# Two buffers for the shifted copies and banded weights of a convolution on TensorE, its steps placed differently among the projection tiles

## The chip, the core and the metric

The kernel runs on one core of one Trainium2 chip. The metric is the device time of one execution in microseconds (us). Before the change the median of three runs is 1551.79 us (1549.15 to 1553.39).

## The reference

One inference step of a two-layer encoder for 512 prompt frames and 8 x 16 sample frames, 640 columns in all. Layer 0 is a convolution module and a SwiGLU block; layer 1 projects keys and values, attends, and has a SwiGLU block too. The change touches the convolution module:

```python
def conv_module(h, hist, g, w_pw1, b_pw1, w_dw, b_dw, ln_g, ln_b, w_pw2, b_pw2):
    a, gate = jnp.split(rms_norm(h, g) @ w_pw1 + b_pw1, 2, axis=-1)
    glu = a * jax.nn.sigmoid(gate)
    full = jnp.concatenate([hist.astype(glu.dtype), glu], axis=1)
    y = lax.conv_general_dilated(
        full, w_dw[:, None, :].astype(full.dtype), window_strides=(1,), padding="VALID",
        dimension_numbers=("NWC", "WIO", "NWC"), feature_group_count=D_MODEL) + b_dw
    y = jax.nn.silu(layer_norm(y, ln_g, ln_b))
    return h + y @ w_pw2 + b_pw2, full[:, -CONV_HIST:]
def swiglu_ffn(h, g, w_in, w_out):
    a, b = jnp.split(rms_norm(h, g) @ w_in, 2, axis=-1)
    return h + (jax.nn.silu(a) * b) @ w_out
```

The model width is 1024 (8 chunks of 128 channels), the convolution has 31 taps for each channel, all arrays are float32.

## The kernel before

**Columns and products.** Channels lie on the 128 partitions, frames on the free axis. The 640 columns are two groups: g0 with 256 (the samples and the first 128 prompt frames) and g1 with 384. A float32 product is made of three matmuls (`mm3`, lines 167 to 172): weights and data are split into a high and a low part, and L170 is high by high, L171 low weights by high data, L172 high weights by low data. A weight tile (2048 columns, 1 MB) is loaded by SyncE (SP) into `raw` (L134, L139); ScalarE (ACT) makes its high part `whi` (L150), and VectorE (DVE), GpSimd (POOL) or both make its low part `wlo` (L154). `raw`, `whi` and `wlo` have two buffers each.

**Steps.** The order of the first part of layer 0 is the string `PLAN` (line 70). A loop at the end of the quoted code runs its tokens through `step`:

- aN, bN: tile N of the first projection for g0 or g1: two accumulations of 24 matmuls, 256 or 384 columns wide; then tanh and bias on ACT (L380, L383) and the gated product on DVE, written with the history to `gs` (g0) or `gp` (g1, L395).
- lgN, pgN: chunk N of the convolution of group g on TensorE (PE). l makes the banded weights `w4` on POOL (L444), copies the chunk to DRAM (`sc`, L452) and reads it back as four shifted copies `x4` by four DMAs of SP (L455, 368 KB each for g0). p is 32 groups of four small matmuls (L469) and a copy to `y` on ACT (L471).
- dg..: chunks convolved on DVE, one instruction for each tap (L434 for the first, L437 for the others), with the sums in PSUM and a copy to `y` on ACT (L440).
- qgN: a chunk convolved on ACT (L416) and POOL (L417).
- ng: the layer norm of the convolution. POOL adds seven chunks (L195), PE makes the sum over the partitions (L204), DVE copies it, PE spreads it over the partitions (L216); L483 subtracts the mean. Squares (L179) are added in the same way, L226 and L230 make the reciprocal root, PE spreads it again, L489 scales, L491 is the silu on ACT, and L159 and L160 split the result into the high and low data of the second projection.
- wg: the second projection, four weight tiles, 192 matmuls for g0; L506 adds to `h`.
- rg: the norm ahead of the SwiGLU block. For g0: squares, POOL sums, the sum on PE, L226, L230, the spread, then L243 (DVE), L159 and L160 for each of 8 chunks.
- f: one chunk of that block for g0, six input tiles (`ffn_in`; L287 silu, L288 product, L160) and the output tiles (`ffn_out`, L303). With a weight tile of f, POOL makes three quarters of `wlo` and DVE one quarter.
- x, y, s: norm and load of g1, and a store of the new history.

The five p steps are chunks 4, 5, 7 and 6 of g0 (in this order) and chunk 3 of g1.

**Who sets the order.** Each engine runs its instructions in its own order. The tile framework's scheduler makes that order from the code's order, with priorities (the blocks under `high_priority`) and a simulated timeline; so an engine's order follows `PLAN` only in the large. The pools wait for buffers: a tile with one buffer can't be written until the last reader of the tile before it has ended. `w4` and `x4` are in pool `cp`, which has one buffer for a tag. PSUM has four buffers for accumulations.

Of the kernel before, what the change touches and what calls it, by code (L numbers as in the profile page):

```python
# [8 lines left out]
F32 = mybir.dt.float32  # L9
# [5 lines left out]
P = 128  # L15
# [14 lines left out]
GSW = 16 * SEG + 4  # L30
# [36 lines left out]
FG = (1, 0)  # L67
SSQ1 = 'ppapappp'
LNO = ((1, 5, 4, 3, 6, 0, 2, 7), (3, 5, 6, 4, 2, 7, 1, 0))
PLAN = ("a0 y a1 a2 a4 x a3 a5 a6 l04 p04 l05 d0213 a7 b0 p05 b1 l07 p07 l06 b2 q00 s0 p06 n0 b3 b4 b5 d145 l13 w0 b7 r0 p13 b6 f q16 s1 d101 d127 n1 f f w1 r1")  # L70

V_NCONV, V_BPW1, V_BDW, V_LNG, V_LNB, V_BPW2 = 0, 8, 24, 32, 40, 48
V_NKV, V_NATT, V_NFFN, V_NFIN, V_N = 56, 64, 72, 88, 96
# [4 lines left out]
def tile_trunk(ctx, tc, xT, vecs, hist, w_pw1, w_pw2, w_in0, w_out0, w_in1, w_out1,  # L78
# [13 lines left out]
    def nm(s):  # L92
        uid[0] += 1
        return f"{s}_{uid[0]}"
# [241 lines left out]
    cp = cv.enter_context(tc.tile_pool(name="cp", bufs=1))  # L336
# [19 lines left out]
    for b in range(2, 4):  # L356
        nc.gpsimd.tensor_tensor(out=i4, in0=i4, in1=ident[:, 32 * b:32 * b + 32], op=ALU.add)
    y0 = hp0.tile([P, 2 * CM * 256], F32, tag="hid0", name="y0")
    y = [y0[:, 0:KT * 256].rearrange("p (k n) -> p k n", k=KT),
         cp.tile([P, KT, 384], F32, name="y1", tag="y")]  # L360
# [79 lines left out]
            nc.scalar.activation(out=y[g][:, c, :], in_=sts[i], func=AF.Copy)  # L440

    def conv_pe_load(c, g):
        w4 = cp.tile([P, 32, 32], F32, tag="w4", name=nm("w4"))
        nc.gpsimd.tensor_tensor(  # L444
            out=w4, in0=i4[:, None, :].to_broadcast([P, 32, 32]),
            in1=dwv[:, V_DW4 + 32 * c:V_DW4 + 32 * c + 32].unsqueeze(2).to_broadcast([P, 32, 32]),
            op=ALU.mult)
        full = GSW if g == 0 else GPW
        wd = full - 4
        src = gsf if g == 0 else gp  # L450
        sc = dr.tile([P, GSW], F32, tag="sc", name=nm("sc"))
        nc.sync.dma_start(sc[:, 0:full], src[:, c, :])  # L452
        x4 = cp.tile([P, 4, GSW], F32, tag="x4", name=nm("x4"))
        for s in range(4):
            nc.sync.dma_start(x4[32 * s:32 * s + 32, :, 0:wd],  # L455
                              sc[:, s:s + wd].rearrange("(q p) w -> p q w", q=4))
        return w4, x4
# [60 lines left out]
    def step(op, arg):  # L518
        g, cs = int(arg[:1] or 0), [int(c) for c in arg[1:]]
        if op == "a":  # L520
            if g < 2:
                glu(g, 0, *(w00, w01)[g])
            else:
                pw1(g, 0)
        elif op == "b":
            pw1(g, 1)
        elif op == "y":
            load_x(1)
        elif op == "x":
            xs[1] = rms(1, V_NCONV, SSQ1, 8)  # L530
        elif op == "l":
            x4s[g, cs[0]] = conv_pe_load(cs[0], g)
        elif op == "p":
            conv_pe(cs[0], g, *x4s[g, cs[0]])
        elif op == "q":
            conv_pool(cs[0], g)
        elif op == "d":
            conv(cs, g)
        elif op == "s":
            if g == 0:  # L540
                nc.sync.dma_start(convs_out, gs[:, :, 0:8, :])
            else:
                nc.sync.dma_start(convp_out, gp[:, :, 384:384 + HIST])
        elif op == "n":
            zs[g] = conv_ln(g)
        elif op == "w":
            pw2(g, zs[g])
        elif op == "r":
            late[g] = (R0, R1)[g](g, V_NFFN)
        elif op == "f":  # L550
            ffn({0: hp0}, w_in0, w_out0, {0: late[0]}, (0,), (chunks.pop(0),), PFA)

    for tok in PLAN.split():
        step(tok[0], tok[1:])
# [39 lines left out]
    for b in range(4):  # L594
        for hh in range(2):
            r0 = b * 32 + hh * 16
# [488 lines left out]
    for q in range(2):  # L1085
        for k in range(KT):
            x = xg[k // 4][:, k % 4, TH[q]]
# [184 lines left out]
```

## Time and profile before

| | |
|---|---|
| median of the runs | 1551.79 us (1549.15, 1551.79, 1553.39) |
| the profiled execution | 1551.3 us, span of the trace 1549.5 us |
| mean clock granted to PE | 0.984 |
| PE busy | 1471.7 us, 95% of the span |
| DVE busy | 1050.1 us, 68% |
| ACT busy | 662.4 us, 43% |
| POOL busy | 443.8 us, 29% |

The span is the time from the first to the last instruction in the trace. A row of the timeline is start, duration, engine, line, operation, the tile written and the tiles read (buffer numbers left out), shapes; what stands in brackets is how long the engine idled before it, and what released it. A row of the table by windows has, for a stretch of the span, its length, the busy time and the number of instructions for each engine, the granted clock of PE (1 is full), the share of the DMA engines that were busy and the GB/s.

### The profile page before, as it was taken

The numbers are of one execution on the slowest core, as the hardware profiler recorded it, in microseconds if no ns is written. First come the engines' busy times: TensorE is split into PE (matmuls) and PEld (weight loads), VectorE is DVE, ScalarE is ACT, GpSimd is POOL, SyncE is SP. The second block draws the span as 40 slices with busy tenths as digits, with TensorE's granted clock in tenths as the row PEclk, the third lists the DMA queues.
The fourth block names the chain that finished last, engine by engine and source line by source line (L and its number), as shares of the span: only waits on it lengthen the run. The fifth ranks groups of instructions, "written<-read, shape, count | busy, mean of one in ns | idle before, by whom it ended". The sixth has DMA issues, their size and how long they took to land.

```text
span 1549.5 us, 26569 instructions
## 1 busy us (share of the span) xinstructions
PE 1471.7 (95%) x10770; PEld 1398.9 (90%) x10770; DVE 1050.1 (68%) x1863; ACT 662.4 (43%) x1173; POOL 443.8 (29%) x403
## 2 busy tenths in 40 slices
PE   5888998989999999999999999999989999999997
PEld 5878888989999999999988798886989999999997
DVE  6994999988555455457576767566796476476455
ACT  4544454535423323235454445443554244244244
POOL 6865568877501000001321211110411121121110
PEclk9999999999999999999999999998999999999998
DMA  7784434444421333433655545453103213213211
GB/s 236 234 228 142 137 113 159 148 157 153 147 82 55 129 116 129 135 118 126 202 183 201 174 140 205 133 175 114 55 28 109 82 56 109 82 55 109 82 55 68
DMA packets 59658, 199.95 MB, mean 129 GB/s; under 512 B 10128, under 2 KB 22672, under 8 KB 46736
## 3 DMA queue, kind: packets, MB, share of 16 engines
q1 hardware_dynamic: 59248, 197.96, 39.1%
q8 instruction: 84, 1.38, 0.4%
q10 hardware_dynamic: 288, 0.31, 0.1%
q14 instruction: 38, 0.31, 0.1%
HBM read 187.02 MB, written 11.22 MB: 128 GB/s over the span
## 4 chain that ended last, share of the span: by engine, by line
PE 71%; DVE 16%; ACT 3%; issue 3%; DMA 3%; POOL 2%; SPq 0%; POOLq 0%; DVEq 0%; ACTq 0%
PE mm L170 12%; PE mm L172 12%; PE mm L171 12%; PE pb L968 6%; DVE w L437 5%; DVE wlo L154 4%; PE pc L968 4%; PE pa L968 4%; PE pb L170 1%; PE pb L171 1%; PE pb L172 1%; PE pa L172 1%; PE pa L170 1%; PE pc L170 1%; PE pc L172 1%
## 5 line engine op out<-in xcount | busy, mean ns | idle before, releaser
L171 PE MATMUL mm<-x,wlo 128*128 128x256 f32 (+1 forms) x1344 | 416.8, 312 | 15.4 <-DVE wlo L154 14.9
L170 PE MATMUL mm<-x,whi 128*128 128x256 f32 (+1 forms) x1344 | 413.3, 312 | 6.4 <-ACT x L159 3.7
L172 PE MATMUL mm<-x,whi 128*128 128x256 f32 (+1 forms) x1344 | 412.7, 311 | 0.5
L150 ACT ACTIVATE whi<-raw 128x2048 fp32r<-128x2048 f32 (+2 forms) x117 | 197.7, 1694 | 232.6 <-PE mm L172 138.8
L171 PEld LDWEIGHTS mm<-x,wlo 128*128 128x128 f32 x1344 | 257.1, 192 | 18.7 <-DVE wlo L154 17.5
L170 PEld LDWEIGHTS mm<-x,whi 128*128 128x128 f32 x1344 | 254.5, 191 | 11.2 <-ACT x L159 4.1
L172 PEld LDWEIGHTS mm<-x,whi 128*128 128x128 f32 x1344 | 255.1, 191 | 2.9 <-DVE x L160 1.8
L154 DVE TENSOR_TENSOR wlo<-raw,whi 128x2048 fp32r<-128x2048 f32 (+5 forms) x117 | 214.0, 1832 | 62.2 <-ACT whi L150 61.2
L154 POOL TENSOR_TENSOR wlo<-raw,whi 128x1536 fp32r<-128x1536 f32 (+3 forms) x50 | 145.7, 2918 | 69.0 <-ACT whi L150 69.0
L913 POOL TENSOR_TENSOR raw<-raw 128x512 f32<-128x512 f32 x38 | 50.5, 1330 | 332.3 <-DVE raw L913 257.5
L171 PE MATMUL mm<-hid,wlo 128*128 128x256 f32 (+1 forms) x352 | 107.7, 308 | 6.6 <-DVE wlo L154 6.6
L172 PE MATMUL mm<-hid,whi 128*128 128x256 f32 (+1 forms) x352 | 105.8, 307 | 0.2
L170 PE MATMUL mm<-hid,whi 128*128 128x256 f32 (+1 forms) x352 | 104.6, 307 | 0.1
L437 DVE SCALAR_TENSOR_TENSOR w<-gp,dwv,w 128x384 f32<-128x384 f32 x180 | 103.9, 612 | 0.8
L195 POOL TENSOR_TENSOR acc<-sq,sq 128x384 f32<-128x384 f32 (+1 forms) x8 | 8.1, 1006 | 258.2 <-ACT sq L179 258.1
L171 PEld LDWEIGHTS mm<-hid,wlo 128*128 128x128 f32 x352 | 66.0, 188 | 7.8 <-DVE wlo L154 7.8
L417 POOL TENSOR_TENSOR y<-y,cvt 128x256 f32<-128x256 f32 (+1 forms) x60 | 69.3, 1154 | 6.3 <-ACT cvt L416 4.0
L172 PEld LDWEIGHTS mm<-hid,whi 128*128 128x128 f32 x352 | 65.7, 188 | 0.6 <-DVE hid L160 0.6
L159 ACT ACTIVATE whi<-raw 128x1024 fp32r<-128x1024 f32 x38 | 39.4, 1054 | 61.6 <-PE pc L172 18.1
L170 PEld LDWEIGHTS mm<-hid,whi 128*128 128x128 f32 x352 | 65.2, 188 | 0.4 <-ACT hid L159 0.3
L968 PE MATMUL pa<-x0f,whi 128*128 128x320 f32 x228 | 61.2, 316 | 2.5 <-DVE t L913 2.3
L195 POOL TENSOR_TENSOR acc<-acc,sq 128x384 f32<-128x384 f32 (+1 forms) x48 | 52.7, 1097 | 28.9 <-ACT sq L179 27.5
(317 smaller groups left out, 3391.4 us busy)
## 6 DMA issues: line engine op xcount, KB each, us to landing
raw<-in_w_in SPq DMA_DIRECT2D x62, 1024.0 KB
raw<-in_w_out SPq DMA_DIRECT2D x36, 768.0 KB
raw<-in_w_pw SPq DMA_DIRECT2D x22, 1024.0 KB
cache<-in_ck SPq DMA_DIRECT2D x32, 512.0 KB
cache<-in_cv SPq DMA_DIRECT2D x32, 512.0 KB
raw<-in_w_kq SPq DMA_DIRECT2D x8, 1024.0 KB
x<-sc SPq DMA_DIRECT2D x16, 368.0 KB
raw<-in_w_out SPq DMA_DIRECT2D x4, 1024.0 KB
```

Source lines behind the costliest of these rows:

```text
L150: nc.scalar.activation(out=hi[:, a:b], in_=raw[:, a:b], func=AF.Copy)
L154: eng.tensor_tensor(out=lo[:, a:b], in0=raw[:, a:b], in1=hi[:, a:b].bitcast(F32), op=ALU.subtract)
L159: nc.scalar.activation(out=hi, in_=src, func=AF.Copy)
L170: nc.tensor.matmul(ps, wh, xh, start=(i == 0), stop=False)
L171: nc.tensor.matmul(ps, wl, xh, start=False, stop=False)
L172: nc.tensor.matmul(ps, wh, xl, start=False, stop=(i == last))
L195: last["acc"] = eng.tensor_tensor(out=acc[:, :n], in0=prev, in1=s(), op=ALU.add)
L417: nc.gpsimd.tensor_tensor(out=y[g][:, c, :], in0=y[g][:, c, :], in1=pr[:, :n], op=ALU.add)
L437: nc.vector.scalar_tensor_tensor(out=dst, in0=src, scalar=wj, in1=dst, op0=ALU.mult, op1=ALU.add)
L913: ENG[e].tensor_tensor(out=out, in0=a, in1=b, op=op)
L968: nc.tensor.matmul(ps, a[:, c], b[:, k, :], start=(first and k == 0 and i == 0), stop=(k == 3 and i == 2), skip_group_check=not first)
```

## The change

`w4` and `x4` get two buffers each, so that the load of a chunk waits for the p before the last one, not for the last. In `PLAN`, l04 stands before a6; p04 moves behind a7, the eighth projection tile of g0; p05 stays behind b0, with the next load before it; the last two chunks change places (6 then 7; before 7 then 6); and b7, a projection tile of g1, moves from behind w0 to ahead of it. All else is the same.

```diff
-PLAN = ("a0 y a1 a2 a4 x a3 a5 a6 l04 p04 l05 d0213 a7 b0 p05 b1 l07 p07 l06 b2 q00 s0 p06 n0 b3 b4 b5 d145 l13 w0 b7 r0 p13 b6 f q16 s1 d101 d127 n1 f f w1 r1")
+PLAN = ("a0 y a1 a2 a4 x a3 a5 l04 a6 l05 d0213 a7 p04 b0 l06 p05 b1 l07 p06 b2 q00 s0 p07 n0 b3 b4 b5 d145 l13 b7 w0 r0 p13 b6 f q16 s1 d101 d127 n1 f f w1 r1")
-        w4 = cp.tile([P, 32, 32], F32, tag="w4", name=nm("w4"))
+        w4 = cp.tile([P, 32, 32], F32, tag="w4", name=nm("w4"), bufs=2)
-        x4 = cp.tile([P, 4, GSW], F32, tag="x4", name=nm("x4"))
+        x4 = cp.tile([P, 4, GSW], F32, tag="x4", name=nm("x4"), bufs=2)
```

The order of the instructions moves on every engine. Three places follow.

On PE, at the first sum of n0 (L204), before the change (`mm_202` is b4; b3 is complete ahead of these rows):

```order
L171 MATMUL mm_202_1512<-x_62_499,wlo_201_1508 128x384
L172 MATMUL mm_202_1512<-x_62_499,whi_200_1507 128x384
L204 MATMUL w2_168_1345<-onec_80,acc_169_1346 128x1 x2
L204 MATMUL w2_168_1345<-onec_80,y0_106 128x1 x2
L170 MATMUL mm_202_1512<-x_62_499,whi_200_1507 128x384
```

and after it (`mm_196` is the second accumulation of b3):

```order
L170 MATMUL mm_196_1476<-x_62_499,whi_193_1445 128x384
L171 MATMUL mm_196_1476<-x_62_499,wlo_194_1446 128x384
L172 MATMUL mm_196_1476<-x_62_499,whi_193_1445 128x384
L204 MATMUL w2_168_1345<-onec_80,acc_169_1346 128x1 x2
L204 MATMUL w2_168_1345<-onec_80,y0_106 128x1 x2
L170 MATMUL mm_196_1476<-x_62_499,whi_193_1445 128x384
```

Before, 53 matmuls of b3 and b4 stand between the last p of g0 and the sum, and after, 42 of b3; from the sum to the spread it is 22 both times.

On PE, at the second spread of n0 (L216) and the start of w0 (data `x_183`), before (`mm_210` is b5):

```order
L172 MATMUL mm_210_1598<-x_62_499,whi_207_1568 128x384
L204 MATMUL w2_171_1370<-onec_80,acc_173_1373 128x1 x2
L216 MATMUL w2_171_1370<-ident_75,rst2_182_1399 128x128 x2
L170 MATMUL mm_220_1709<-x_183_1403,whi_218_1703 128x256
L171 MATMUL mm_220_1709<-x_183_1403,wlo_219_1704 128x256
```

and after (`mm_221` is b7 here; the sum stands 33 matmuls of b7 ahead of the spread, behind its first 15):

```order
L170 MATMUL mm_221_1734<-x_62_499,whi_218_1703 128x384
L171 MATMUL mm_221_1734<-x_62_499,wlo_219_1704 128x384
L172 MATMUL mm_221_1734<-x_62_499,whi_218_1703 128x384
L216 MATMUL w2_171_1370<-ident_75,rst2_182_1399 128x128 x2
L170 MATMUL mm_227_1771<-x_183_1403,whi_225_1765 128x256
L171 MATMUL mm_227_1771<-x_183_1403,wlo_226_1766 128x256
```

The tile b7, 48 matmuls, now stands ahead of the spread, and the first matmul of w0 still follows it at once. Behind w0 the rows before were b7, r0's sum, 20 of p13's 32 groups, r0's spread, 12 of p13's, b6, f; now they are p13, 26 of b6, r0's sum, 22 of b6, r0's spread, f, and the first two input tiles of f stand interleaved.

On POOL, from r0's root (L230) to the weights of the third input tile of f, before (`wlo_276`, `wlo_283`, `wlo_290` are the first three input tiles of f; L417 is q16):

```order
L230 TENSOR_TENSOR rst2_255_2029<-rst_254_2027,mhalf_82 128x2
L154 TENSOR_TENSOR wlo_276_2164<-raw_274_2162,whi_275_2163 128x1536
L154 TENSOR_TENSOR wlo_283_2227<-raw_281_2225,whi_282_2226 128x1536
L417 TENSOR_TENSOR y1_107<-y1_107,cvt_336_2729 128x384
L417 TENSOR_TENSOR y1_107<-y1_107,cvt_337_2732 128x384
L154 TENSOR_TENSOR wlo_290_2290<-raw_288_2288,whi_289_2289 128x1536
```

and after (`wlo_276` now stands three rows ahead of L230):

```order
L230 TENSOR_TENSOR rst2_255_2029<-rst_254_2027,mhalf_82 128x2
L154 TENSOR_TENSOR wlo_283_2227<-raw_281_2225,whi_282_2226 128x1536
L417 TENSOR_TENSOR y1_107<-y1_107,cvt_336_2729 128x384
L417 TENSOR_TENSOR y1_107<-y1_107,cvt_337_2732 128x384
L417 TENSOR_TENSOR y1_107<-y1_107,cvt_338_2735 128x384
L417 TENSOR_TENSOR y1_107<-y1_107,cvt_339_2738 128x384
L417 TENSOR_TENSOR y1_107<-y1_107,cvt_340_2741 128x384
L195 TENSOR_TENSOR acc_369_2951<-y1_107 128x384
L417 TENSOR_TENSOR y1_107<-y1_107,cvt_341_2744 128x384
L417 TENSOR_TENSOR y1_107<-y1_107,cvt_342_2747 128x384
L417 TENSOR_TENSOR y1_107<-y1_107,cvt_343_2750 128x384
L417 TENSOR_TENSOR y1_107<-y1_107,cvt_344_2753 128x384
```

The next row there is `wlo_290`; so nine L417 and one addition stand between the second and the third weight tile of f, where two L417 stood. On POOL the L444 of p13's load also stood between the second and the third addition of n0's first sum, and now it doesn't.

Of the other engines: on DVE the taps of d145 stand further ahead than before, 9 more of them ahead of n0's L489, 13 more ahead of r0's L226, 11 more ahead of each step of the first f, and none from the second input tile of the third f on. On SP, the DMAs of the second and fourth `x4` stand where they did and those of the third one row earlier, but they wait for another buffer. The sum and spread of n1 stand earlier, in the first input tiles of the third f (before behind its second).

## The prediction

> **What bounds the kernel now.** The page's first rows give the busy time of each engine; then the windows show where PE (TensorE) is not full, and the waits say for whom it waits there.
>
> ```profile
> PE 1471.7 (95%) x10770; PEld 1398.9 (90%) x10770; DVE 1050.1 (68%) x1863; ACT 662.4 (43%) x1173; POOL 443.8 (29%) x403
> 43.00:156.00 113.00, 97.72 (x786) 88.33 (x785) 91.17 (x155) 54.65 (x88) 75.60 (x76) 0.94 0.70 202
> 156.00:210.00 54.00, 51.97 (x401) 47.48 (x401) 53.36 (x92) 26.51 (x42) 23.17 (x13) 0.97 0.34 118
> 210.00:332.00 122.00, 104.38 (x833) 100.60 (x832) 121.82 (x194) 59.74 (x78) 104.69 (x54) 0.96 0.47 150
> 332.00:390.00 58.00, 55.13 (x461) 54.20 (x460) 46.45 (x52) 27.93 (x40) 43.59 (x21) 0.99 0.47 160
> 390.00:1549.50 1159.50, 1136.05 (x8107) 1082.85 (x8107) 710.84 (x1332) 472.04 (x892) 166.27 (x193) 0.99 0.35 115
> ```
>
> Behind 390 us PE is busy for 1136.05 of 1159.50 us, and the change moves nothing there: what is won or lost before 390 us carries through to the end. Before it two stretches bind differently. From 156 to 332 us DVE is full (53.36 of 54, 121.82 of 122): there PE, 17.6 us idle in the second of them, follows DVE. From 43 to 156 us DVE is idle for 21.8 us and PE for 15.3: each waits for the other in turn, and the five p steps lie there. The waits of PE, first to 156 us, then from 332 to 390:
>
> ```profile
> PE mm L469 <- DMA x<-sc: 10.5, 2, 5.4
> PE mm L170 <- ACT x L159: 2.6, 1, 2.6
> PE w L216 <- POOL rst L230: 1.4, 1, 1.4
> ...
> PE mm L171 <- DVE wlo L154: 2.7, 2, 1.7
> ```
>
> The largest, 10.5 us in two waits for `x4`, is what the second buffer bears on. It is not all that it costs: PE comes out of the second wait at a lower clock.
>
> ```profile
> 103.81 0.66 PE L469 MATMUL mm<-x,w 128*32 128x256 f32 x4 [5.43 <-DMA x<-sc]
> 118.68 3.67 PE L469 MATMUL mm<-x,w 128*32 128x256 f32 x64 [0.72 <-ACT t L380]
> 98.00:108.00 10.00, 4.57 (x47) 2.42 (x49) 10.00 (x19) 3.25 (x4) 6.17 (x5) 0.66 0.61 155
> ```
>
> Granted 0.66 over 10 us is 3.4 us of full clock lost. [...]
>
> **Part by part. The wait ahead of p04** stays almost whole.
>
> ```profile
> 67.03 1.51 PE L469 MATMUL mm<-x,w 128*32 128x256 f32 x12 [5.11 <-DMA x<-sc]
> 63.23 3.36 DVE L154 TENSOR_TENSOR wlo<-raw,whi 128x1024 fp32r<-128x1024 f32 x1
> ```
>
> PE ended a6 at 67.03 - 5.11 = 61.92. Now a7 stands there, and it needs its low weights: the DVE half of them ends at 63.23 + 3.36 = 66.59, and the rows ahead of it on DVE are the same. So PE waits 4.67 us for `wlo` in place of 5.11 for `x4`: -0.4. It would be -5.1 if `wlo` came early, and 0 at worst.
>
> **The third and fourth p.** The third `x4` was issued only when p05 had read the one before it, and PE waited 5.43. Now it waits for p04 alone, a whole tile of 48 matmuls earlier, and should be there. The 0.72 ahead of p06 goes too. With the clock PE leaves the last p at 122.35 - 5.43 - 0.72 - 3.4 - 0.4 = 112.4. What is late next is the sum of n0:
>
> ```profile
> 121.00 2.30 POOL L195 TENSOR_TENSOR acc<-y 128x256 f32<-128x256 f32 x1 [9.54 <-ACT y L440]
> 124.07 1.92 POOL L444 TENSOR_TENSOR w<-i,dwv 128x1024 f32<-128x1024 f32 x1
> 125.95 3.18 POOL L195 TENSOR_TENSOR acc<-acc,y 128x256 f32<-128x256 f32 x4
> 118.61 0.56 DVE L395 SCALAR_TENSOR_TENSOR gp<-t,t 128x384 f32<-128x384 f32 x1 [1.18 <-ACT t L380]
> 131.57 0.50 PE L204 MATMUL w<-onec,acc 128*128 128x1 f32 x4
> 136.30 0.61 PE L216 MATMUL w<-ident,mst 128*128 128x128 f32 x4
> 117.00:156.00 39.00, 34.26 (x242) 32.20 (x240) 18.72 (x34) 18.11 (x27) 19.78 (x17) 0.95 0.43 137
> 180.73 0.51 PE L170 MATMUL mm<-x,whi 128*128 128x384 f32 x2
> 189.25 0.50 PE L204 MATMUL w<-onec,acc 128*128 128x1 f32 x4
> ```
>
> From 180.73 to 189.25 PE did b7, 48 matmuls: 0.1775 us each. Before the sum now stand 42 of them, 7.5 us: PE is there at 120. POOL's chain hangs on the taps of DVE by way of ACT's copies. DVE's idle time lies behind 117 us (39.00 - 18.72 = 20.3 of the 21.8), so those taps come no earlier than by the 1.18 at L395, behind which the last of them stand. The chain ended at 125.95 + 3.18 = 129.1 and loses L444's 1.92 and DVE's 1.18: 126.0. PE waits about 6 us, then goes at half clock for a while; the 22 matmuls to the spread take 3.9 us warm and 7.8 cold, I take 6. So the spread stands at 132, 4.3 ahead of 136.30, with 11 matmuls (1.95) less done: PE is 2.3 ahead, not the 10 that the waits promise. If POOL's chain came early, it would be up to 9.
>
> **b7 ahead of w0.** The chain into w0, on ACT and PE:
>
> ```profile
> 149.14 0.58 ACT L380 ACTIVATE t<-mm,hb 128x384 f32<-128x384 f32 x1 [1.43 <-PE mm L172]
> 149.62 1.90 ACT L150 ACTIVATE whi<-raw 128x2048 fp32r<-128x2048 f32 x1
> 151.53 1.28 ACT L491 ACT_TABLE_LOAD   x1
> 152.83 1.09 ACT L491 ACTIVATE n<-y,vec 128x256 f32<-128x256 f32 x2
> 153.82 0.71 ACT L159 ACTIVATE x<-n 128x256 fp32r<-128x256 f32 x2
> 154.28 0.58 PE L170 MATMUL mm<-x,whi 128*128 128x256 f32 x1 [2.64 <-ACT x L159]
> ```
>
> From ACT's wake at b5's end, 149.1, to w0 it took 5.2 us, of which PE waited 1.38 for the root and 2.64 for the data (1.4 and 2.6 among the waits). In the new order 33 of b7 cover the root; but ACT has b7's L380, a `whi`, the table and the silu in a row behind b7, as it had them behind b5. From the spread at 132 it is 32 + 48 + 48 matmuls, 22.7 us, to the end of b7 at 154.8; with 5.2 to 6.5 behind it w0 starts at 160 to 161.3, take 161. Before, with b7's 8.5 counted, it was 162.8: PE is 1.8 ahead.
>
> **r0 without b7 in its cover.** w0 takes 180.73 - 154.28 = 26.45, to 187.5; p13 and b6 took from 189.25 to f:
>
> ```profile
> 204.34 0.28 PE L170 MATMUL mm<-x,whi 128*128 128x256 f32 x1
> 197.01 0.87 DVE L243 SCALAR_TENSOR_TENSOR n<-h,vec,w 128x256 f32<-128x256 f32 x2
> 206.42 0.75 DVE L160 TENSOR_TENSOR x<-n,x 128x256 fp32r<-128x256 f32 x2
> L437 DVE SCALAR_TENSOR_TENSOR w<-gp,dwv,w 128x384 f32<-128x384 f32 x180 | 103.9, 612 | 0.8
> ```
>
> That is 15.1 us, so PE could start f at 202.6. r0's sum stood 8.5 us behind w0, and stands 15.1 less 22 matmuls, 11.2, behind it: 198.7 against 189.25, 9.4 later. Its reader on DVE (L226) has 13 more taps ahead of it, 13 x 0.612 = 8.0: 9.4 - 8.0 = 1.4 us of DVE are not covered. Then the eight chunks of x come off DVE from 197.01 to 207.17, 10 us behind a spread that is now at the very start of f. f must go at the pace of x; its first two tiles, interleaved, have just about that much work (96 matmuls of 256 columns, at 256/384 of b7's rate 0.118 us each: 11.4 us). What follows on POOL:
>
> ```profile
> 212.05 2.54 POOL L417 TENSOR_TENSOR y<-y,cvt 128x384 f32<-128x384 f32 x2
> 214.54 3.48 POOL L154 TENSOR_TENSOR wlo<-raw,whi 128x1536 fp32r<-128x1536 f32 x1
> 329.69 0.58 PE L171 MATMUL mm<-x,wlo 128*128 128x256 f32 x1 [3.56 <-DVE wlo L154]
> 326.00:333.00 7.00, 3.44 (x17) 3.31 (x16) 6.96 (x6) 2.79 (x3) 7.00 (x3) 0.76 0.33 96
> ```
>
> The third weight tile's low part began at 214.54; seven more L417 at 2.54 / 2 and one addition put it about 10 us later, less what POOL begins early: PE starts that tile some 6 us later. DVE has 11 more taps (6.7 us) to do there, so it doesn't idle. It has those taps behind it at the third f, where DVE's whole work counts, and that is what the end hangs on: the third f starts 1.4 later by DVE. I take it at +1.4; from -2 (PE's 1.8, if DVE idles nowhere) to +7 (DVE idle while POOL is late). At 329.69 PE waited 3.56 and lost 0.24 x 7 = 1.7 of clock; with PE itself later, half of the clock loss goes: -0.9, from -1.7 to 0. n1's sum and spread come earlier, and of the two waits behind them (2.7) half goes: -1.4, from -2.7 to 0.
>
> **The sum:** +1.4 - 0.9 - 1.4 = -0.9. The leads of 0.4, 2.3 and 1.8 are not in it, since DVE, not PE, sets 210 to 332 us. The profiled execution took 1551.3 us (span 1549.5), within the runs and 0.5 under their median: 1550.4. By the bounds: -6.4 (1544.9) to +7 (1558.3). A measurement of this kernel tells no less than 0.3%, 4.7 us, from no change.
>
> **Rivals.** *The waits for `x4` go and stay gone.* The x4 waits and the clock behind them are 5.1 + 5.4 + 0.7 + 3.4 = 14.6 us. DVE's 20.3 us of idle time lie in the very stretch behind the last p; if POOL's chain is done by 121, b3 to b5 reach DVE some 6 to 9 us earlier, d145 starts that much earlier, and the third f with it: about 1544. For it: the idle is there. Against it: the sum of n0 stands in front of the end of b3. [...] Chance 0.22.
>
> *r0 in the open, slower.* r0's spread ends right at f, and POOL has nine L417 ahead of f's third weight tile. The place is DVE from 200 to 232 us: it is full today, and each us that it idles there, with the product of a tile (L288) waiting for PE, PE for `wlo` and POOL for L417, is lost for good. It decides from 5 us of DVE idle on, and up to the 6 to 10 by which POOL is later: about 1557.5. For it: no slack in the row of 210 to 332. Against it: the 11 taps ahead. Chance 0.21.
>
> *The second buffer doesn't help.* The third `x4` still lands late, since it goes through the same SP queue and DMA engines as the weights (DMA share 0.70 to 156 us); the sum of n0, at which PE has 6 us to spare, takes up the wait. Then b7's move is all that is left: 1551.3, within the same case.
>
> **The numbers.** My forecast, with the last rival, has 0.57; its own range is 1545 to 1556. 1543.5 to 1558.5 takes in most of both other cases. Faster by over 0.3%: 0.22, within: 0.57, slower: 0.21.
>
> **What would show it.** Right: PE's wait for `x4` gone from p06 and p07 and in its place one of 4 to 7 us ahead of L204 for POOL's L195; ahead of a7 a wait of 4 to 5 for `wlo`; w0 at 160 to 162; f's first matmuls held by x, with its third tile at 224 to 228; DVE without idle from 205 to 332; the third f within 2 of 329.7. Wrong: L204 without a wait and b3's L395 before 125 (faster), or DVE idle by over 5 us between 200 and 232 (slower), or a wait for `x4` still ahead of the third p.

## The result

The change is slower: 1559.02 us in the median of 20 runs (1553.12 to 1565.52) against 1551.42 in 20 runs of the kernel before (1546.22 to 1554.24), ratio 1.0056 with a 95% interval of 1.0042 to 1.0069. The profiled execution, 1553.79 us with a span of 1552.0, is one of the fastest of the 20; it shows 2.5 of the 7.6 us. So a second trace was taken (run e1 below, span 1562.8), and both are read here.

The first rows of the page and the table by windows of the first trace (before: 97.72, 51.97 and 104.38 us of PE in the first three windows):

```profile
PE 1466.6 (94%) x10770; PEld 1394.8 (90%) x10770; DVE 1046.7 (67%) x1863; ACT 662.9 (43%) x1173; POOL 443.1 (29%) x403
43.00:156.00 113.00, 103.91 (x841) 94.98 (x839) 91.46 (x167) 58.65 (x91) 78.60 (x80) 1.00 0.73 211
156.00:210.00 54.00, 45.10 (x326) 40.60 (x327) 51.31 (x75) 22.57 (x36) 23.91 (x15) 0.85 0.32 104
210.00:332.00 122.00, 105.53 (x863) 102.51 (x861) 118.55 (x200) 61.32 (x84) 98.26 (x53) 0.96 0.45 146
332.00:390.00 58.00, 52.30 (x440) 50.70 (x440) 46.21 (x55) 32.08 (x46) 41.56 (x18) 1.00 0.47 154
```

Up to 156 us PE gains: 103.91 us busy, 841 matmul records instead of 786, at full clock. From 156 to 210 us it loses more than that: 6.9 us less busy, 326 records instead of 401, and a clock of 0.85 where it was 0.97. The waits of PE in the timeline of the first trace tell where:

```profile
67.62 0.39 PE L171 MATMUL mm<-x,wlo 128*128 128x256 f32 x1 [0.70 <-POOL wlo L154]
122.72 0.38 PE L204 MATMUL w<-onec,acc 128*128 128x1 f32 x2 [0.59 <-POOL acc L195]
156.38 0.58 PE L170 MATMUL mm<-x,whi 128*128 128x256 f32 x1 [4.74 <-ACT x L159]
203.12 0.46 PE L170 MATMUL mm<-x,whi 128*128 128x256 f32 x1 [3.22 <-ACT x L159]
206.95 0.58 PE L171 MATMUL mm<-x,wlo 128*128 128x256 f32 x1 [2.31 <-DVE wlo L154]
223.10 0.38 PE L170 MATMUL mm<-x,whi 128*128 128x256 f32 x1 [1.93 <-ACT whi L150]
227.17 0.58 PE L171 MATMUL mm<-x,wlo 128*128 128x256 f32 x1 [3.57 <-DVE wlo L154]
```

The two waits for `x4` (5.11 and 5.43) are gone, and what was expected in their place, at a7 and at n0's sum, hardly shows (0.70 and 0.59). w0 starts at 156.38 behind a wait of 4.74. Then come the new ones: at f's first tile for its data, 3.22 and 2.31, and at its third tile for weights, 1.93 and 3.57. Before, f ran from 204.34, and its one wait of over half a microsecond in that stretch was 2.12. In the second trace the same places read:

```profile
68.25 0.58 PE L171 MATMUL mm<-x,wlo 128*128 128x256 f32 x1 [4.47 <-DVE wlo L154]
126.32 0.38 PE L204 MATMUL w<-onec,acc 128*128 128x1 f32 x2 [2.49 <-POOL acc L195]
161.55 0.39 PE L170 MATMUL mm<-x,whi 128*128 128x256 f32 x1 [4.74 <-ACT x L159]
205.97 0.39 PE L170 MATMUL mm<-x,whi 128*128 128x256 f32 x1 [3.22 <-ACT x L159]
230.20 0.58 PE L171 MATMUL mm<-x,wlo 128*128 128x256 f32 x1 [3.57 <-DVE wlo L154]
```

Here the waits at a7 and n0's sum are there, 4.47 and 2.49, and w0 starts 5.2 us later. The large waits from w0's start on (4.74, 3.22, 3.57) are the same to the hundredth in both traces: they belong to the order. The early ones differ and belong to the execution.

### The profile page after: what moved, and what is told of

It reads as the page before. It is cut to its first block, busy times and chain, and to the rows that moved or that the text cites. A ratio compares the mean times of both kernels' runs of the same rounds, so it can differ in the third digit from the quotient of the medians.

```text
span 1552.0 us, 26569 instructions
## 1 busy us (share of the span) xinstructions
PE 1466.6 (94%) x10770; PEld 1394.8 (90%) x10770; DVE 1046.7 (67%) x1863; ACT 662.9 (43%) x1173; POOL 443.1 (29%) x403
## 4 chain that ended last, share of the span: by engine, by line
PE 71%; DVE 17%; ACT 3%; DMA 3%; issue 2%; POOL 2%; DVEq 0%; ACTq 0%; POOLq 0%; SPq 0%
PE mm L170 13%; PE mm L171 13%; PE mm L172 13%; DVE w L437 6%; PE pb L968 6%; PE pc L968 4%; PE pa L968 4%; DVE wlo L154 3%; PE pb L170 1%; PE pb L172 1%; PE pb L171 1%; PE pa L172 1%; PE pa L170 1%; PE pc L170 1%; PE pc L172 1%
## 5 line engine op out<-in xcount | busy, mean ns | idle before, releaser
L171 PE MATMUL mm<-x,wlo 128*128 128x256 f32 (+1 forms) x1344 | 417.2, 313 | 17.0 <-DVE wlo L154 15.5
L172 PE MATMUL mm<-x,whi 128*128 128x256 f32 (+1 forms) x1344 | 410.5, 310 | 2.3 <-DVE x L160 2.3
L171 PEld LDWEIGHTS mm<-x,wlo 128*128 128x128 f32 x1344 | 257.3, 192 | 20.7 <-DVE wlo L154 18.2
L172 PEld LDWEIGHTS mm<-x,whi 128*128 128x128 f32 x1344 | 254.0, 191 | 4.3 <-DVE x L160 3.2
L154 DVE TENSOR_TENSOR wlo<-raw,whi 128x2048 fp32r<-128x2048 f32 (+5 forms) x117 | 209.1, 1790 | 69.1 <-ACT whi L150 68.0
L171 PE MATMUL mm<-hid,wlo 128*128 128x256 f32 (+1 forms) x352 | 107.7, 309 | 5.4 <-DVE wlo L154 5.3
L172 PE MATMUL mm<-hid,whi 128*128 128x256 f32 (+1 forms) x352 | 105.9, 307 | 1.3 <-DVE hid L160 1.3
L195 POOL TENSOR_TENSOR acc<-sq,sq 128x384 f32<-128x384 f32 (+1 forms) x8 | 8.1, 1007 | 255.9 <-ACT sq L179 255.8
L171 PEld LDWEIGHTS mm<-hid,wlo 128*128 128x128 f32 x352 | 66.1, 188 | 6.5 <-DVE wlo L154 6.4
L417 POOL TENSOR_TENSOR y<-y,cvt 128x256 f32<-128x256 f32 (+1 forms) x60 | 65.6, 1094 | 13.4 <-ACT cvt L416 10.7
L172 PEld LDWEIGHTS mm<-hid,whi 128*128 128x128 f32 x352 | 65.9, 188 | 1.6 <-DVE hid L160 1.5
L195 POOL TENSOR_TENSOR acc<-acc,sq 128x384 f32<-128x384 f32 (+1 forms) x48 | 52.9, 1102 | 32.5 <-ACT sq L179 28.2
```

What stands on the lines that cost most here:

```text
L154: eng.tensor_tensor(out=lo[:, a:b], in0=raw[:, a:b], in1=hi[:, a:b].bitcast(F32), op=ALU.subtract)
L171: nc.tensor.matmul(ps, wl, xh, start=False, stop=False)
L172: nc.tensor.matmul(ps, wh, xl, start=False, stop=(i == last))
L195: last["acc"] = eng.tensor_tensor(out=acc[:, :n], in0=prev, in1=s(), op=ALU.add)
L417: nc.gpsimd.tensor_tensor(out=y[g][:, c, :], in0=y[g][:, c, :], in1=pr[:, :n], op=ALU.add)
```

## The experiments

Each run was timed beside the kernel before on the same chip; the ratios are to that. e1 to e4 shared one set of runs of before (median 1551.11), e5 to e8 another (1550.91), e9 to e12 a third (1548.08), e13 to e16 (1550.93) and e17 with e18 (1550.85).

**e1, the change again.** 

> The changed kernel once more, for a second trace. Its 20 runs lie from 1553.1 to 1565.5 us, and the only trace (1553.8) is one of the fastest, so it shows 2.5 us of the 7.6 that the medians differ by. Theory A (r0's chain and the first tiles of f lie open since b7 no longer covers them): a slower execution shows more PE idle time and half clock between 199 and 230 us than the 12 us of idle time of the first trace. Rival B (the third or fourth set of shifted copies lands late in the slower executions): the extra idle time lies at L469, before 123 us, where the first trace has 0.46. Rival C (the first load of the program, 1.6 us later in the trace after than before, carries it all): the first matmul at 14.5 us or later and everything behind it only shifted. All three expect a median of 1557 to 1561.

Measured: 1560.36 us (1555.46 to 1564.62), ratio 1.0059 (1.0037 to 1.0080). The two traces are 3.6 us apart at n0's sum, 5.2 at w0, 3 at f, 8.5 at the end of the third f, and 10.8 in the span. Theory A's extra idle time between 199 and 230 us isn't there (from 200 to 232 us PE is busy for 20.18 and 19.82 us), B's L469 doesn't wait at all, and for C the start differs by 0.2 us only. These two traces part at the early waits (how the one at a7 comes about is told at the end) and again in the third f, which takes 60.6 us in the first and 65.6 in the second. Why the third f differs was not found.

**e2, the convolution part alone; e16, the same again.**

```diff
-PLAN = "... d145 l13 b7 w0 r0 p13 b6 f ..."
+PLAN = "... d145 l13 w0 b7 r0 p13 b6 f ..."
```

> The change without the move of b7 (w0 stands ahead of b7 again; two buffers and the moved p and l steps stay). Theory A: the loss is b7's; what is left is the gain of the convolution part, PE 6.8 us ahead at the first spread of n0 (127.5 against 136.3, with 11 matmuls of 0.18 us less done), of which DVE, full from 156 to 332 us, passes on the part by which n0's chain starts earlier: 1544 to 1549 us, ratio 0.995 to 0.999. Rival B (late copies): about as slow as the whole change, 1557 to 1561.

> e2 once more: 1544 to 1549 us, ratio 0.995 to 0.999. Its trace, if a7's low weights arrive 4 us late this time, shows PE waiting at n0's sum for POOL and the later milestones 6 to 8 us behind e2's first trace; if not, the same milestones within 1.5 us.

Measured: 1546.36 us (1542.26 to 1558.36), ratio 0.9975 (0.9954 to 0.9995), and 1546.85, ratio 0.9980 (0.9964 to 0.9996). This is the fastest version found, and faster than the kernel before both times, by some 4.5 us (both intervals end just below 1). The trace of e2 waited 0.81 us at n0's sum. That of e16 waited longer, though its a7 was only 0.72 late, and stands 6.2 us behind e2's at n0's second L226, so the expectation named too narrow a cause:

```profile
125.89 0.37 PE L204 MATMUL w<-onec,acc 128*128 128x1 f32 x1 [3.51 <-POOL acc L195]
```

**e3, the move of b7 alone**, in the kernel before.

```diff
-PLAN = "... d145 l13 w0 b7 r0 p13 b6 f ..."
+PLAN = "... d145 l13 b7 w0 r0 p13 b6 f ..."
```

> The kernel before with b7 ahead of w0 and nothing else. Theory A: this alone costs more than the whole change, since it also loses the lead of the convolution part: 1558 to 1566 us, ratio 1.004 to 1.010, with waits of PE for x (L159, L160) at the start of f and for the third weight tile of f. Rival B: 1550 to 1553.

Measured: 1561.84 us (1560.30 to 1565.75), ratio 1.0075 (1.0050 to 1.0100). b7's move, with all that the scheduler makes of it, is the loss: 10.7 us alone, 12.4 on top of the convolution part (1559.02 less 1546.6). Its waits are those of the change:

```profile
163.79 0.58 PE L170 MATMUL mm<-x,whi 128*128 128x256 f32 x1 [4.74 <-ACT x L159]
209.19 0.39 PE L170 MATMUL mm<-x,whi 128*128 128x256 f32 x1 [3.22 <-ACT x L159]
228.59 0.38 PE L170 MATMUL mm<-x,whi 128*128 128x256 f32 x1 [1.92 <-ACT whi L150]
232.66 0.58 PE L171 MATMUL mm<-x,wlo 128*128 128x256 f32 x1 [3.57 <-DVE wlo L154]
```

w0 starts at 163.79, which is 1.0 us late: before it was 154.28, and b7's 8.5 us now stand ahead. f starts 4.9 us late (209.19 against 204.34), and its third tile 13.6 (232.66 against 219.07 in the timeline of before).

**e4, the buffers alone; e10, the convolution part's order without them.**

```diff
 e4: w4 and x4 with bufs=2, PLAN of before
 e10: e2's PLAN, w4 and x4 with one buffer
```

> The kernel before with the second buffers of w4 and x4 alone, PLAN as it was. It parts the second buffer from the order. The wait of 5.11 us ahead of p04 should stay, since p04 still stands behind a6, and the one of 5.43 ahead of the third p go. Theory A: 1546 to 1551 us, ratio 0.997 to 1.000. Rival B: slower than before, 1555 or more.

> Run e2 (convolution part of PLAN, b7 behind w0) with one buffer for w4 and x4. Theory K (the second buffer is needed by the new order: p05's copies now wait for p04, which stands one tile later): PE waits for x4 ahead of p05, 5 us or more, and again ahead of p06: 1551 to 1558 us. Rival L (order alone makes the gain of e2, the buffer is idle): 1545 to 1548.

Measured: e4 1549.67 us (1545.60 to 1554.01), ratio 0.9993 (0.9978 to 1.0009), no change; e10 1561.40 (1558.83 to 1564.48), ratio 1.0084 (1.0059 to 1.0109). In e4 the wait ahead of the third p stays, in e10 there is one ahead of p05:

```profile
105.00 0.66 PE L469 MATMUL mm<-x,w 128*32 128x256 f32 x4 [6.11 <-DMA x<-sc]
```

```profile
93.82 0.65 PE L469 MATMUL mm<-x,w 128*32 128x256 f32 x4 [8.01 <-DMA x<-sc]
```

The expectation that the second buffer alone takes the wait at the third p away was wrong: SP's order there is the store of the history, `sc`, then the load of b3's weights, which waits for a `raw` buffer, and only then the copies. K holds in kind, with a time above its 1551 to 1558: with the new order the buffer is needed, 15 us are between e10 and e2. Neither half is worth anything alone.

The second buffer also has a cost that the working left out. With it POOL makes two `w4` at the very start, and one of the additions of the first norm (L195) on DVE takes longer beside them: 2.12 us in the first trace of the change, where a later one takes 0.42. POOL and DVE before, then in e4:

```profile
5.98 1.95 POOL L444 TENSOR_TENSOR w<-i,dwv 128x1024 f32<-128x1024 f32 x1 [3.28 <-DMA dwv<-in_vecs]
8.13 1.40 DVE L195 TENSOR_TENSOR acc<-acc,sq 128x256 f32<-128x256 f32 x3
```

```profile
5.87 4.01 POOL L444 TENSOR_TENSOR w<-i,dwv 128x1024 f32<-128x1024 f32 x2 [3.18 <-DMA dwv<-in_vecs]
8.04 3.11 DVE L195 TENSOR_TENSOR acc<-acc,sq 128x256 f32<-128x256 f32 x3
```

The first matmul comes at 12.9 to 13.0 us in every trace with one buffer and at 14.4 to 14.8 in every trace with two. How much of these 1.4 to 1.9 us reaches the end was not tried.

**e7, the last two chunks not swapped.**

```diff
-PLAN = "... l06 p05 b1 l07 p06 b2 q00 s0 p07 n0 ..."
+PLAN = "... l07 p05 b1 l06 p07 b2 q00 s0 p06 n0 ..."
```

> Run e2 (convolution part alone, 1546.4 us) with the last two chunks back in the order 7, 6. In e4 the third set of shifted copies came as late as before (wait 6.11 us) though it had its own buffer: on SP its DMAs stand behind the load of b3's weights, which waits for a raw buffer. In e2 they stand ahead of that load. Theory H (SP's order, made by the swap, removes this wait, and the second buffer only allows it): the wait of 5 to 6 us is back and most of the gain of e2 goes, 1549 to 1552 us. Rival I (the second buffer and p04's place make the gain): 1545 to 1548, no wait at the third p.

Measured: 1549.60 us (1541.89 to 1554.73), ratio 0.9991 (0.9975 to 1.0006). The size is H's, but the mechanism isn't shown: in the trace the third p waits 2.78 us for ACT (L380), not for copies, and the span is 1540.1. The intervals of e7 and e2 overlap; what the swap is worth stays open.

**e5 and e9, a third pair of weight buffers for f's third tile**, in e3's kernel and in the kernel before.

```diff
+        nth[0] += 1
+        own = nth[0] == 23
+        pl, hn, ln = (cp, "whi3", "wlo3") if own else (wp, "whi", "wlo")
-XPAD, WPAD, OPAD, HPAD = 0, 40, 16, 16
+XPAD, WPAD, OPAD, HPAD = 0, 0, 16, 16
-        x4 = cp.tile([P, 4, GSW], F32, tag="x4", name=nm("x4"))
+        x4 = cp.tile([P, 4, GSW - 4], F32, tag="x4", name=nm("x4"))
```

> Run with b7 alone moved (e3, 1561.8 us) with one addition: the third weight tile of f has buffers of its own for whi and wlo (padding elsewhere cut to make room). In e3 PE waits 1.92 and 3.57 us for that tile (228.6 and 232.7 us) and then runs at half clock for 6.8 us. Theory D: the first two tiles of f run interleaved, so both pairs of weight buffers come free only at the end of both, and the third tile can't be split before; with its own buffers these waits go and half of the cold time: 5.5 + 3.4 less 1 to 3 that DVE takes back, 1553 to 1557 us. Rival E (POOL's nine L417 hold the tile up, which stay where they are): no change, 1560 to 1563. Rival F (PE is held by DVE's taps, whatever the weights do): 1560 to 1563, with the wait moved to another instruction of the same tile.

> Control of e5: the kernel before with the third weight tile of f in buffers of its own and the same padding cut. e5 came to 1566.3 us, slower than e3 (1561.8); in its trace the two waits ahead of f's third tile are gone and the first f ends 5.0 us sooner than in e3 (278.7 against 283.7), but from the end of the second f on it loses 11 us in stages that the change doesn't touch. Theory D (the buffers do what was said, the padding cut costs the later stages): this control is 4 to 10 us slower than before, 1555 to 1561, and the time is lost behind 390 us. Rival E (the buffer itself only moves the wait): 1549 to 1553.

Measured: e5 1566.25 us (1563.57 to 1569.90), ratio 1.0103 (1.0083 to 1.0123); e9 1567.54 (1563.49 to 1570.53), ratio 1.0122 (1.0096 to 1.0148). e5 is slower than all three of its expectations. The waits at f's third tile did go, but PE then waited 5.82 us for the data in place of 3.22. The control lost in the stages behind the third f, as D said, but in the first f too: 274.3 at its end against 268.4. With this buffer b7's move costs nothing (1566 against 1568) because the control is spoilt as well. In the traces the two stand only 2.3 us apart at the end of the second f (336.2 and 333.9), where e3 and the kernel before stand 8.1 apart; but with a control whose own first f is 5.9 us late, nothing can be read from the pair on the cause.

**e6, b6 ahead of w0; e11, p13 ahead of w0; e8, b7 behind p13**, each in e2's kernel.

```diff
-PLAN = "... l13 w0 b7 r0 p13 b6 f ..."
+e6:  PLAN = "... l13 b6 w0 b7 r0 p13 f ..."
+e11: PLAN = "... l13 p13 w0 b7 r0 b6 f ..."
+e8:  PLAN = "... l13 w0 r0 p13 b7 b6 f ..."
```

> The whole change, but b6 in place of b7 stands ahead of w0, and b7 behind it. The cover between the end of w0 and f is the same 14 us as in the change (one tile and p13, where before and e2 have two tiles and p13), but r0's sum stands one tile behind w0 as in the kernel before, and q16, which needs b6, can run some 35 us earlier. Theory A (it is the amount of cover between w0 and f): as slow as the change, 1557 to 1561 us. Rival E (q16's work on ACT and POOL beside f's first weights): 1546 to 1551. Rival G (r0's sum placed late, behind 26 matmuls of the last tile): 1546 to 1552.

> Run e2 with p13 in place of b7 ahead of w0: p13, w0, b7, r0, b6, f. PE's work between the end of w0 and f is b7 and b6, 17.1 us, against 22.6 in e2 and 14.1 in the change. Theory A (the time lost goes with the cover that r0's chain lacks, some 13.5 us at f's third tile for 8.5 us of cover): about half to two thirds of b7's cost, 1551 to 1558 us, with a wait for x ahead of f of 1 to 3 us and f's first two tiles interleaved. Rival M (it is b7, its ACT work in the chain into w0): 1545 to 1548.

> Run e2 with b7 moved the other way, behind p13: w0, r0, p13, b7, b6, f. r0's sum stands 5.7 us behind w0 and 46 us of... its spread has b7 and b6, some 17 us, between itself and f. Theory A (cover between r0's spread and f is what counts): as fast as e2 or faster, 1541 to 1547 us, no wait of PE for x at f. Rival J (b7 next to w0 is what counts, since b7's gated product feeds the taps of d127 or the sum now waits for POOL): a new wait of PE ahead of r0's sum and 1548 to 1554.

Measured: e6 1560.42 us (1557.42 to 1564.95), ratio 1.0069 (1.0049 to 1.0088); e11 1560.36 (1555.13 to 1562.49), ratio 1.0072 (1.0046 to 1.0098); e8 1551.80 (1546.71 to 1559.32), ratio 1.0017 (0.9998 to 1.0036). Whichever piece of work is taken from behind w0 and put ahead of it, the kernel is as slow as the change, so the loss doesn't need b7, q16's time or the place of r0's sum. The trace of e11 has the change's waits at f's third tile, 1.93 and 3.57. e6 is weaker evidence: inside its w0 PE waits 7.4 us for weights in six waits, where the change has one of 2.10. The loss is not in proportion either: p13 (5.6 us) costs as much as b7 (8.5), more than was expected for e11. And more work between r0's spread and f (e8) gains nothing; it is slower than e2, with a wait of 1.30 ahead of r0's sum in its trace, so A's expectation for it failed. Time and wait are those that J named, but 1.30 us is too little for the 5.2 between e8 and e2; why it is slower was not settled.

**e12, a7's low weights on DVE alone**, in e2's kernel.

```diff
-PL1 = ((0, 2, 2, 2, 2, 2, 2, 2), ...
+PL1 = ((0, 2, 2, 2, 2, 2, 2, 0), ...
```

> Run e2 with the low weights of a7 made by DVE alone (PL1 0 for that tile; half by POOL in all others). Traces come in two kinds: a7's low weights arrive 0.7 us late (after, e2, e6, e7) or 4 us late (e1, e8), by whether DVE's subtraction or its x L160 begins behind POOL's and then takes until POOL's ends (1.6 or 3.4 us). Theory N (this collision makes the spread of the runs, 16 us in e2): without POOL's half the slow kind goes, 1542 to 1547 us, spread under 10. Rival O (DVE, which has no idle time there, pays 1.1 us more and other collisions take its place): 1546 to 1552, spread as before.

Measured: 1561.65 us (1558.88 to 1564.50), ratio 1.0089 (1.0063 to 1.0116), worse than both expected. The scheduler moved n0's sums with it, and PE waited 8.03 us for POOL at the second. It doesn't tell N from O.

**e13, e14, e15: the two visible consequences of b7's move taken back**, in the changed kernel. e13 queues f's second tile behind the first on PE, e14 queues b6 behind r0's sum, e15 does both.

```diff
 e13, e15:
-                ffn_in(w_in, j0 + jj, xs, hid, jj, groups, pl)
+                if groups == (0,) and j0 + jj == 1:
+                    with tc.issue_after(mmi[0].ins):
+                        ffn_in(w_in, j0 + jj, xs, hid, jj, groups, pl)
+                else:
+                    ffn_in(w_in, j0 + jj, xs, hid, jj, groups, pl)
 e14, e15:
-            pw1(g, 1)
+            if g == 6:
+                with tc.issue_after(last["sum"].ins):
+                    pw1(g, 1)
+            else:
+                pw1(g, 1)
```

> The whole change, with PE's matmuls of f's second tile queued behind the first tile's (nothing else changed in the code; the first tile has its weight buffers free earlier). Theory D (the interleaving is the cause): the waits of 1.9 and 3.6 us ahead of the third tile and the cold clock there go, 5 to 8 us faster than the change: 1551 to 1555 us. Theory P (r0's late sum is the cause; f's first tile runs at the pace of the data until 220 us whatever stands beside it): the time moves from one wait to the other, 1557 to 1561.

> The whole change, with PE's matmuls of b6 queued behind r0's sum, which so stands right behind p13, 26 matmuls (4.6 us) earlier. Theory P: the sum at about 190.5 instead of 195.0 in the first trace, the data of f 4 to 5 us earlier, of which f's waits take that much less: 1553 to 1556 us. Theory D (the tiles are still interleaved): 1557 to 1561. Third case Q (PE waits at the sum for POOL's squares, 2 us or more): 1556 to 1559 with that wait.

> e13 and e14 together. If each takes away a cost of its own, 8 to 12 us faster than the change: 1547 to 1551 us. If both are one cost (the lacking cover), no faster than the better of the two, 1553 to 1556.

Measured: 1560.01 us, ratio 1.0059 (1.0041 to 1.0077); 1558.33, ratio 1.0056 (1.0036 to 1.0075), PE waiting 2.20 us at the sum for POOL as in case Q; 1555.63 (1552.57 to 1560.62), ratio 1.0033 (1.0018 to 1.0047). In e13 the waits at the third tile are gone and stand at the first, where f's data come no sooner: D fell. Alone neither gives anything that can be told; together 3.4 us against the change, with intervals that still overlap (1.0018 to 1.0047 against 1.0042 to 1.0069). The time is that of one cost, 1553 to 1556, though it is better than either alone.

**e17, n1 back in its place; e18, with e15 on top.** In the change n1's sum stood in the first tiles of the third f; before, behind the second.

```diff
-PLAN = "... d101 d127 n1 f f w1 r1"
+PLAN = "... d101 d127 f f w1 r1"
                 ffn_in(w_in, j0 + jj, xs, hid, jj, groups, pl)
+                if groups == (0,) and j0 + jj == 13:
+                    with tc.issue_after(mmi[0].ins):
+                        zs[1] = conv_ln(1)
```

> The whole change, with n1 written behind the second tile of the third f and its matmuls queued behind that tile, where they stood in the kernel before. Theory R (the early n1 brings its squares and sums on ACT, POOL and DVE into the tiles of the third f and costs 1 to 5 us there): 1554 to 1558 us, the third f back at 59.5 to 60.5. Rival S (the prediction's: the early n1 saves waits, 1.4 us): 1559 to 1562.

> e15 (b6 behind r0's sum, f's first tiles in sequence; 1555.6 us) with n1 as in e17. If R holds and the three are separate: 1551 to 1554 us, near the kernel before and still 5 above e2, which is then what the missing tile of cover costs by itself. If S: 1555 to 1558.

Measured: e17 1553.93 us (1549.79 to 1557.97), ratio 1.0021 (1.0007 to 1.0034), 5.1 us faster than the change with intervals that don't overlap; e18 1559.94 (1556.48 to 1564.54), ratio 1.0066 (1.0043 to 1.0090). R holds in e17, whose trace is a twin of e1's up to the third f; the third f then takes 59.4 us against 65.6. In the first trace of the change, with n1 early too, it takes 60.6, so what the early n1 costs depends on the execution. The table by windows for the third f, e1 and then e17:

```profile
334.00:402.00 68.00, 59.81 (x475) 57.66 (x474) 55.65 (x60) 35.44 (x47) 46.93 (x20) 0.97 0.44 143
```

```profile
334.00:402.00 68.00, 64.24 (x516) 62.36 (x515) 52.47 (x58) 35.04 (x47) 49.50 (x20) 1.00 0.49 161
```

PE is busy 4.4 us more in the same 68, 516 records instead of 475, and the clock stays at 1.00. What it waited for in e1, and in e17, in that window:

```profile
PE mm L171 <- DVE wlo L154: 3.5, 3, 1.4
PE mm L170 <- DVE h L303: 1.6, 1, 1.6
PE mm L172 <- DVE hid L160: 1.3, 1, 1.3
```

```profile
PE mm L173 <- DVE wlo L154: 1.7, 2, 1.0
PE mm L174 <- DVE hid L160: 0.7, 1, 0.7
```

(L173 and L174 of e17 are L171 and L172.) e18 shows that the pieces don't add: there n1 came to stand among other matmuls, PE waited 2.79 us at its spread, and the third f took 68.7 us.

The stages in the traces, as starts on DVE in us (f1 to f3 are the first three f, each by its last L303):

| | before | e2 | e16 | change | e1 | e3 | e15 | e17 |
|---|---|---|---|---|---|---|---|---|
| n0's second L226 | 149.6 | 142.7 | 148.9 | 146.4 | 151.6 | 153.8 | 149.7 | 151.6 |
| r0's L226 | 190.6 | 183.8 | 190.5 | 198.2 | 201.0 | 204.3 | 196.0 | 200.7 |
| first L288 of f | 215.2 | 208.4 | 215.0 | 221.9 | 224.8 | 228.0 | 218.6 | 224.4 |
| f1 | 268.4 | 261.9 | 267.2 | 276.5 | 279.5 | 283.7 | 272.4 | 279.3 |
| f2 | 330.1 | 322.6 | 327.3 | 331.1 | 334.6 | 338.2 | 329.4 | 334.0 |
| f3 | 389.8 | 382.9 | 387.3 | 391.7 | 400.2 | 400.3 | 391.4 | 393.4 |
| span | 1549.5 | 1541.2 | 1544.6 | 1552.0 | 1562.8 | 1559.5 | 1552.7 | 1554.1 |

## Why the prediction was wrong

1. **The wait ahead of p04.** "PE waits 4.67 us for `wlo` in place of 5.11": 4.47 in the second trace, 0.70 in the first. The step holds for one execution and is too dear for the other.

2. **The third and fourth p, and the sum behind them.** The waits for `x4` went. A wait for POOL's sum in their place was right in kind: 6 us forecast, 0.59, 2.49, 3.51 (e16) and 3.75 (e17) measured, and 0.81 in e2; the spread was forecast at 132 and stood at 127.5 and 132.7. From the sum to the spread the working took 6 us, between 3.9 at full and 7.8 at half clock; it was 4.8 in the first trace, behind the wait of 0.59 and with a granted clock of 1.00 from 123 to 128 us, and 6.4 in the second, behind 2.49. Half clock is what the trace of before has around the end of its wait of 5.43: 0.50 from 101 to 107.6 us, with PE starting again at 103.81. What the working ascribed to the buffer was the order of SP as much (e4, e10), and the later start that comes with the buffer (e4) was put at nothing. All told the convolution part gives 4.5 us (e2, e16). Of this the sum had nothing: "The leads of 0.4, 2.3 and 1.8 are not in it".

3. **b7 ahead of w0.** w0 was forecast at 160 to 161.3; it started at 156.38 and 161.55, with the chain over ACT behind b7 as described (the wait of 4.74 is in the change, e1, e3 and e17 alike; e10, where b7 stays behind w0, has it too, so b7 is not what makes it).

4. **r0 without b7 in its cover.** This is the step that failed, in its size: "9.4 - 8.0 = 1.4 us of DVE are not covered", and so "the third f starts 1.4 later by DVE". The places were right: f at the pace of its data, the first two tiles interleaved, the third at 224 to 228 (227.17 and 230.20). The credit came in as well: at f1 DVE has 11 taps more behind it than without the move, 6.7 us of work, and by f2 all but one are made up for. But the delay was larger than the working had it. f1 is 15.3 us late in e3 against before, and 12.1 in e17 against e16; f2, where the third f starts, is still 8.1 and 6.7 late, in place of 1.4.

   Two things on DVE made it larger. First, its own instructions took longer. In the new order b6's L395 and f's data (L160) run beside POOL's work; DVE before, then DVE and POOL in the first trace:

```profile
208.19 0.55 DVE L395 SCALAR_TENSOR_TENSOR gp<-t,t 128x384 f32<-128x384 f32 x1
```

```profile
202.92 2.85 DVE L395 SCALAR_TENSOR_TENSOR gp<-t,t 128x384 f32<-128x384 f32 x1
201.91 3.44 POOL L154 TENSOR_TENSOR wlo<-raw,whi 128x1536 fp32r<-128x1536 f32 x1 [2.78 <-ACT whi L150]
216.45 1.12 DVE L160 TENSOR_TENSOR x<-n,x 128x256 fp32r<-128x256 f32 x1
218.66 1.16 DVE L160 TENSOR_TENSOR x<-n,x 128x256 fp32r<-128x256 f32 x1
```

   This L395 and four of the eight L160 (1.0 to 1.2 us in place of 0.4) are as long in e1, e3, e13 and e17, and none is in the traces of before and e16: some 5 us of DVE while f's data are made, which the working put at nothing. Second, DVE waited. Up to the end of f2 it idled 5.0 us more in e3 than before (44.1 and 39.1) and was busy 3.1 more (294.5 and 291.4), so part of those 5 us is won back behind f1; in e17 against e16 the two are 2.1 and 4.5. One of these waits is for PE, 1.73 us at an L303 near the end of f2 in e3. That PE, idle for 17.6 of 122 us before, had too little room to catch up is argued from it, and no run took either of the two things away by itself.

   The second rival, "r0 in the open, slower", gave 1557.5, but its mechanism did not come. It asked for DVE idle by over 5 us between 200 and 232 us, and DVE is busy there for all but 0.14 and 0.25 us in the two traces of the change:

```profile
200.00:232.00 32.00, 20.18 (x126) 19.20 (x127) 31.86 (x48) 17.16 (x31) 22.72 (x15) 0.73 0.29 70
200.00:232.00 32.00, 19.82 (x123) 18.55 (x123) 31.75 (x51) 17.67 (x30) 20.50 (x14) 0.76 0.20 40
```

   Nor do POOL's nine L417 hold up f's third tile. ACT makes its high part behind the silu (L287) of the first product, and the product comes at the end of two interleaved tiles; the timeline of ACT in the first trace:

```profile
220.87 0.38 ACT L287 ACTIVATE t<-mm 128x256 f32<-128x256 f32 x1 [0.68 <-PE mm L172]
221.15 1.90 ACT L150 ACTIVATE whi<-raw 128x2048 fp32r<-128x2048 f32 x1
223.21 1.91 ACT L150 ACTIVATE whi<-raw 128x2048 fp32r<-128x2048 f32 x1
```

   POOL's idle time of 1.36 us ahead of its `wlo` at 223.13 is for that `whi`. But e13 shows that without this wait the same time is lost at the first tile: f's data are late, whatever stands around them.

5. **n1's sum and spread earlier.** The sum had -1.4 for it. By the medians e17 puts it at +5.1: the sign was wrong. In single traces the price runs from about 1 to 6 us (the third f at 60.6 and 65.6 against 59.4). That the earlier chain crowds the tiles there is argued from the two windows at e17; which of n1's instructions costs most was not tried.

6. **The clock at the third f.** The working had half of the clock's loss go. The wait at 329.69 went too, in both traces, and the granted clock from 326 to 333 us is 1.00 where it was 0.76. e2 and e16 keep the wait (3.46 and 3.56), so this small gain comes with b7's move.

Of b7's 12.4 us, 5.1 come back with n1 in its old place (e17), and e17 is still 7.3 above e2 and e16; in the traces f2 is 6.7 late. This is not a division of the cost, since the pieces don't add: with n1 back and both visible consequences undone (e18) the kernel is as slow as the change. That what remains is the lacking cover itself, 14.1 us of PE's work between w0 and f where there were 22.6, is only argued: e11 and, with its own waits, e6 fit it, e8 does not.

The change as a whole is its two halves: 4.5 gained and 12.4 lost. The forecast had nothing for the first, and -0.9 for the second with the third f's terms (+1.4 - 0.9 - 1.4). It missed both in opposite directions, so the errors partly cancel in the total, and that the second rival's number is only 1.5 us off is luck, since DVE did not idle where it said.

## What to carry to other kernels

Work that is moved to cover one dependent chain is taken from another: before moving it, list what runs beside the chain at the old place, and price that chain with the work gone at every engine that is nearly full in the stretch (here DVE, busy for 121.82 of 122 us, and PE, for 104.38), not at the fullest alone. Ask also what each instruction will newly run beside: its duration can change, as L395's did (0.55 us before, 2.85 in the change). Work done ahead pays back a delay only by its own amount: here 6.7 us of a delay of 12 to 15. A second buffer is of use only with an issue order that reaches it early: here the buffers alone gave nothing, the order alone lost some 13 us, and both together won 4.5.

## What the runs showed of the hardware

The executions of the changed kernel differ by up to 12 us, and a part of it goes with which of two instructions is first. Both traces of the change run the same instructions at 58 and 64 us; DVE, then POOL, in the first:

```profile
57.84 0.57 DVE L160 TENSOR_TENSOR x<-n,x 128x384 fp32r<-128x384 f32 x1
62.33 1.58 DVE L154 TENSOR_TENSOR wlo<-raw,whi 128x1024 fp32r<-128x1024 f32 x1
```

```profile
58.43 2.71 POOL L154 TENSOR_TENSOR wlo<-raw,whi 128x1024 fp32r<-128x1024 f32 x1
64.82 2.75 POOL L154 TENSOR_TENSOR wlo<-raw,whi 128x1024 fp32r<-128x1024 f32 x1
```

and in the second, e1:

```profile
58.17 2.65 DVE L160 TENSOR_TENSOR x<-n,x 128x384 fp32r<-128x384 f32 x1
64.84 3.36 DVE L154 TENSOR_TENSOR wlo<-raw,whi 128x1024 fp32r<-128x1024 f32 x1
```

```profile
58.02 2.40 POOL L154 TENSOR_TENSOR wlo<-raw,whi 128x1024 fp32r<-128x1024 f32 x1
64.78 2.34 POOL L154 TENSOR_TENSOR wlo<-raw,whi 128x1024 fp32r<-128x1024 f32 x1
```

In the first, DVE's two instructions are over before POOL's begin and take 0.57 and 1.58 us; in the second they begin 0.15 and 0.06 us behind POOL's, and last until POOL has ended (60.4 and 67.1) and 0.4 and 1.1 us more: 2.65 and 3.36. Together that is 3.9 us of DVE, and a7's low weights come 0.70 us late in the first trace and 4.47 in the second. It is not all of the difference: in e16 and e17 a7 waited for 0.72 and 0.73 us, and n0's sum was late even so. Why DVE's two take longer there was not shown; the rows give only the times. e12, which was to take this collision away, changed the order besides and tells nothing on it.
